# Two gate chunks of the latent branch as one block with seven products in six of its pairs

## The chip, the cores and the metric

The kernel runs on one core of one Trainium2 chip. The metric is the device time of one execution in microseconds (us). Three runs of the kernel before give a median of 1937.64 us (1937.38 to 1937.88). The engines are TensorE (PE, with its weight loads as PEld), VectorE (DVE), ScalarE (ACT), GpSimd (POOL) and SyncE (SP), which issues most loads.

## The reference

The kernel is one layer of a bidirectional encoder on 256 rows of width 4096, in float32. One projection `w_in` gives everything that the two attention branches need; each branch has 16 heads of width 128.

```python
h = rms_norm(x, g_mix[i])
proj = jnp.einsum('bsd,de->bse', h, w_in[i])
c_q, c_kv, k_rope, gate_a, q_b, k_b, v_b, gate_b = jnp.split(proj, split_idx, axis=-1)
q_a = jnp.einsum('bsr,re->bse', rms_norm(c_q, g_q_latent[i]), w_uq[i])
...
kv = jnp.einsum('bsr,re->bse', rms_norm(c_kv, g_kv_latent[i]), w_ukv[i])
...
y_a = rms_norm(y_a.reshape(B, S, MLA_WIDTH), g_out_mla[i]) * jax.nn.silu(gate_a)
...
y_b = rms_norm(y_b.reshape(B, S, DIL_WIDTH).astype(x.dtype), g_out_dil[i]) * jax.nn.silu(gate_b)
x = x + jnp.einsum('bse,ed->bsd', jnp.concatenate([y_a, y_b], axis=-1), w_out[i])
ple = jnp.einsum('bsc,cd->bsd', p[i], w_ple[i])
gate = jax.nn.sigmoid(jnp.einsum('bsd,de->bse', rms_norm(x, g_ple[i]), w_ple_gate[i]))
x = x + ple * gate
```

Between the lines stand the latent attention (a rotary part of 64 columns, a dense softmax) and the dilated attention. `gate_a`, 2048 columns, is what the change is about.

## The kernel before

**Products in three passes.** Each float32 operand is split into a high and a low half (`split`, L112: ScalarE copies the high half at L115, VectorE subtracts for the low half at L116). `mm` (L130) makes one product of three matrix instructions, high by high, high by low, low by high (L133 to L135). The 256 rows are two halves t of 128. A weight chunk of 512 columns and 4096 rows is 32 row blocks (kt) of 128.

**Steps.** The matrix work is a list `steps`, in the order in which TensorE gets it. Each step has a load (SP), a split, and its products. An `Old` step is two row blocks of a chunk of up to 512 columns, for both halves of the rows: 12 matrix instructions. The main loop at the end issues, for each step i, the loads up to a few steps ahead, the splits (`convert`) up to two steps ahead (more where a block has a ring of more than three buffers), then the products of step i, and then calls `advance`.

**Tasks beside the steps.** What is not a weight product is a generator that is taken on by one `yield` per step in `advance`: first the list `urgent` (evacuations, statistics, gating), in the order of spawning, then up to five `running` attention heads. A head waits in `waiting` until its flag is set and two steps have passed since the last start. All engines work in program order, so what a task issues stands in each engine's queue between the splits of that step and those of the next.

**Blocks with seven products.** `Block` (L729) handles 1024 columns at once as a 2 by 2 product of halves of the rows and halves of the columns. Two row blocks (a pair) make either two plain steps, with four products per row block, or one fast pair of four steps: seven products per pair instead of eight, with sums of the weights made by VectorE at L780 and L796, and with sums of x prepared by `add_sums` (L812). The products collect in eight PSUM banks: M2, X, M3, M4 take the plain steps too, M1, M5, M6, M7 only the fast ones. When the last fast pair is done, a `mid` task combines M1, M5, M6, M7; when the last step is done, a `done` task adds M2, X, M3, M4. The order `CCCCSCSCSCSCSCSC` has a letter for each pair, C plain and S fast. The six dilated blocks (q, k, v, twice) and others use this already; the sums `x_s` for the dilated blocks are made late, after the latent heads.

**The order around the change.** First come four chunks of 400 columns (the latents and the rotary key, 64 steps, `done_a`); the last of them spawns `latents`, which turns the rotary key, and the flag "latents" is set when the latents are normalised. Then come gate chunk 0 (16 steps), and eight groups of eight steps: one step of gate chunk 1, four of `w_uq` (two heads' q), one of gate chunk 1, two of `w_ukv` (two heads' k and v). `done_uq` (L472) reads the PSUM banks of `w_uq` at L478, turns the rotary part on GpSimd and transposes it (L488); its last part sets the flag ("uq", i). `done_uk` (L498) reads k at L511 and v at L118 and L119, and puts two heads in `waiting`. `w_uq` and `w_ukv` share one pair of banks.

**A latent head** (`attend`, L386) takes nine steps: transposes of q and k (L393, L394), the split of both, the scores (ten matrix instructions into bank s, L133 to L135, L408, L409), the maximum and exponentials (L415, L417), the normalisation (L433, L438), transposes (L443), their split, the weighted sum into bank o, and its reading (L456, L458). Of the two heads of a group, this text calls the first A and the second B.

**The gate.** `done_gate` (L546) reads a finished gate chunk: a tanh (L550) and a product (L551) for each half of the rows. It then waits for the branch's 1/rms (`ry`, set by `y_stats` when all heads are done), scales, transposes (L564) and multiplies with the heads' outputs (L572). Chunks 2 and 3 of the gate follow the eight groups, 32 steps; in them the last heads end, `y_stats` and the gating run, and `x_sums` makes the sums of x for the dilated blocks.

Of the kernel before, what the change touches and what calls it, by code (L numbers as in the profile page):

```python
# [12 lines left out]
F32R = mybir.dt.float32r  # L13
I32 = mybir.dt.int32
AF = mybir.ActivationFunctionType
ALU = mybir.AluOpType
AX = mybir.AxisListType

P = 128
S = 256  # L20
NT = S // P
DM = 4096
HEADS = 16
# [6 lines left out]
OFF_GA = Q_LORA + KV_LORA + ROPE  # L30
# [48 lines left out]
def encoder_layer(ctx: ExitStack, tc: tile.TileContext, x, p, positions, g_mix, w_in, g_q_latent, w_uq,  # L79
                  g_kv_latent, w_ukv, g_out_mla, g_out_dil, w_out, w_ple, g_ple, w_ple_gate, g_final,  # L80
                  c_inv, c_dist, out):
    nc = tc.nc
    x, p, out = x[0], p[0, 0], out[0]
# [10 lines left out]
    def slot(tag, shape, dtype=F32):  # L94
        names[tag] = names.get(tag, 0) + 1
        return sp.tile([P, *shape], dtype, tag=tag, name=f"{tag}_{names[tag]}")
# [137 lines left out]
    flags, urgent, waiting, running = set(), [], [], []  # L234
    ticks = [0, -9]

    def spawn(task):
        urgent.append(task)
# [66 lines left out]
    T7 = {}  # L305
# [166 lines left out]
    def done_uq(i):  # L472
        def task(ps):
            q = slot("T5", [NT, 2, NOPE + ROPE])
            kq = slot("T6", [1024])
            pairs[i] = {"q": q, "kq": kq}
            for t in range(NT):
                nc.scalar.activation(q[:, t].rearrange("p h c -> p (h c)"), ps[t], AF.Copy, scale=rqs[:, t:t + 1])  # L478
            both = kq[:, 512:].rearrange("p (t h d r) -> p t h d r", t=NT, h=2, d=2)
            rotate(both[:, :, :, 0], q[:, :, :, NOPE:], both[:, :, :, 1], 2)  # L480
            yield
            yield
            nc.scalar.activation(both[:, :, :, 1], both[:, :, :, 0], AF.Copy)
            yield
            tp = turn_bank([2, S])
            for h in range(2):
                for t in range(NT):
                    nc.tensor.transpose(tp[:, h, t * P:(t + 1) * P], both[:, t, h].rearrange("p d r -> p (d r)"),  # L488
                                        ident)
            yield  # L490
            pe = slot("Q0", [2, S], F32R)
            nc.scalar.activation(pe, tp, AF.Copy)
            nc.vector.tensor_tensor(pe[ROPE:], tp[ROPE:], plain(pe[ROPE:]), op=ALU.subtract)
            pairs[i]["pe"] = pe
            flags.add(("uq", i))
        return task
# [28 lines left out]
    def lhs_c(key):  # L525
        return lambda kt: (cT[key][0][:, kt], cT[key][1][:, kt])
# [5 lines left out]
    def y_stats(dil):  # L532
        while not all(("head", dil, h) in flags for h in range(HEADS)):
            yield
        yield
        tp = turn_bank([2 * S])
        for t in range(NT):
            nc.tensor.matmul(tp[:, t:t + 1], acc[:, t * P:(t + 1) * P], ones, start=True, stop=True)
        yield
        yield from rsqrt_mean(ry[dil], tp[:, :NT], WIDTH)  # L540
        nc.vector.tensor_tensor(ry[dil], ry[dil], rxh, op=ALU.mult)
        flags.add(("ry", dil))

    U_TAGS = ("B7a", "B7b", "T5", "T6"), ("T7", "B7a", "B7b", "T4")

    def done_gate(dil, c):  # L546
        def task(ps):
            u = slot(U_TAGS[dil][c], [NT, 512])
            for t in range(NT):
                nc.scalar.activation(u[:, t], ps[t], AF.Tanh, scale=rxh[:, t:t + 1])  # L550
                nc.vector.scalar_tensor_tensor(u[:, t], u[:, t], 1.0, ps[t], op0=ALU.add, op1=ALU.mult)  # L551
                yield
            while ("ry", dil) not in flags or (c and ("turned", dil, c - 1) not in flags):
                yield
            yield
            for t in range(NT):
                nc.scalar.activation(u[:, t], u[:, t], AF.Copy, scale=ry[dil][:, t:t + 1])
            yield
            for b in range(2):
                w = u[:, :, S * b:S * (b + 1)]  # L560
                tp = turn_bank([2, S])
                for k in range(2):
                    for t in range(NT):
                        nc.tensor.transpose(tp[:, k, t * P:(t + 1) * P], w[:, t, k * P:(k + 1) * P], ident)  # L564
                if b:
                    flags.add(("turned", dil, c))
                yield
                for k in range(2):
                    h = 4 * c + 2 * b + k
                    g = G["ob" if dil else "oa"][:, h:h + 1]  # L570
                    y = yb_rows(h) if dil else by_token(y_rows(ya, h))
                    nc.vector.scalar_tensor_tensor(by_token(w[:, k]) if dil else y, y, g, by_token(tp[:, k]),  # L572
                                                   op0=ALU.mult, op1=ALU.mult)
            if not dil:
                flags.add(("gated", c))
                return
            while (("yT", 0, 3) if c == 0 else ("yT", 1, 1)) not in flags and c != 1:
                yield
            if c == 2:
                yt = [slot(b, [4, S], F32R) for b in ("B7a", "T6")]  # L580
            else:
                both = slot({0: "B3", 1: "B5", 3: "B6"}[c], [2, 4, S], F32R)
                yt = [both[:, 0], both[:, 1]]
            yT[4 + c] = yt
            for b in range(2):
                yield
                split(*(q[:, 2 * b:2 * b + 2] for q in yt), u[:, :, S * b:S * (b + 1)])
            flags.add(("yT", 1, c))
        return task

    def split_ya():
# [124 lines left out]
    WP = ["wp"] * 3  # L716
# [92 lines left out]
                Step(None, lambda hi, lo: split(hi, lo, T[1]), run(("M6", S(1)), ("M4", A22)), needs, 0),  # L809
            ]  # L810

    def add_sums(n, pair, dst, tmp, name, out):  # L812

        def task():
            def two(op, d, a, b):
                nc.vector.tensor_tensor(d, a, b, op=op)

            w = slot(tmp, [2, 8, P])  # L820
            for j in range(n):
                a, u = w[:, j % 2, :4], w[:, j % 2, 4:]
                hi, lo = (q.rearrange("p k (t c) -> p (k t) c", t=NT) for q in pair(j))
                two(ALU.add, a, plain(hi), plain(lo))
                two(ALU.add, u[:, 0], a[:, 1], a[:, 3])
                two(ALU.subtract, u[:, 1], u[:, 0], a[:, 0])
                two(ALU.subtract, u[:, 2], a[:, 1], a[:, 0])
                two(ALU.subtract, u[:, 3], a[:, 2], u[:, 1])
                yield
                d = dst(j)  # L830
                split(d[:, 0], d[:, 1], u)
                out[j] = [(d[:, 0, i], d[:, 1, i]) for i in range(4)]
                flags.add((name, j))
                yield
        return task()


# [249 lines left out]
    def banks():  # L1087
        turn[0] ^= 1
        return M[turn[0]]
# [3 lines left out]
    def add(ch, lo=0, hi=None):  # L1093
        steps.extend((ch, j) for j in range(lo, ch.nk // ch.per if hi is None else hi))

    def cols(w, lo, n):
        return w[:, lo:lo + n]

    def from_x(lo, n, done):
        return Chunk(cols(w_in, lo, n), 32, n, lhs_x, banks(), done)  # L1100

    for i in range(4):
        add(from_x(400 * i, 400, done_a(i)))
    add(from_x(OFF_GA, 512, done_gate(0, 0)))
    ga1 = from_x(OFF_GA + 512, 512, done_gate(0, 1))
    other = banks()
    for i in range(8):
        add(ga1, 2 * i, 2 * i + 1)
        add(Chunk(cols(w_uq, 384 * i, 384), 8, 384, lhs_c("q"), other, done_uq(i), lambda j: ["latents"]))
        add(ga1, 2 * i + 1, 2 * i + 2)  # L1110
        add(Chunk(cols(w_ukv, 512 * i, 512), 4, 512, lhs_c("kv"), other, done_uk(i), lambda j: ["latents"]))
    for c in (2, 3):
        add(from_x(OFF_GA + 512 * c, 512, done_gate(0, c)))
    hooks = {}
    EVEN, ODD = ("m0", "m1", "s", "o", "m2", "m3", "t0", "t1"), ("m2", "m3", "t0", "t1", "m0", "m1", "s", "o")
    LAST = "m2", "m3", "s", "o", "m0", "m1", "t0", "t1"
# [1 line left out]
    def mix(shape):  # L1118
        n = shape.count("S")
        fast, plain_ = iter(range(n)), iter(range(n, 16))  # L1120
        return [("ple", 0) if x == "e" else ("fast", next(fast)) if x == "S" else ("plain", next(plain_)) for x in shape]
# [18 lines left out]
    def hook(at, f):  # L1140
        assert at not in hooks
        hooks[at] = f

    def only(*tags):
        def go():
            turns[:] = tags
        return go

    x_s = {}
    z_tags = "T0", "T1", "T2", "T3", "T4", "T7"  # L1150

    def x_sums():
        while ("ry", 0) not in flags:
            yield
        yield from add_sums(6, lambda j: [q[:, 2 * (j % 4):2 * (j % 4) + 2] for q in xT[j // 4]],
                            lambda j: slot(z_tags[j], [2, 4, P], F32R), "B0", "x_sums", x_s)

    hook(64 + 16 + 64, lambda: spawn(y_stats(0)))
    hook(64 + 16 + 64 + 12, lambda: spawn(x_sums()))
    gated_rings = {("T4", "T7"): ("mid", ("k", 1)), "Al1": ("y_sums", FAST_O - 1)}  # L1160
    for n, key in enumerate((key, i) for i in range(2) for key in "qkv"):
        off = {"q": OFF_Q, "k": OFF_K, "v": OFF_V}[key[0]] + 1024 * key[1]
        order = mix("CCCCSCSCSCSCSCSC" if n < 5 else "CCCCCSCCSCCSCCSC")
# [202 lines left out]
    for i, step in enumerate(steps):  # L1366
# [23 lines left out]
        n = 0  # L1390
# [33 lines left out]
```

## Time and profile before

| | |
|---|---|
| median of three runs | 1937.64 us |
| the profiled execution | 1936.72 us |
| its span, first to last instruction | 1934.9 us |
| mean granted TensorE clock | 0.998 |
| VectorE busy | 1449.5 us (75%) |
| ScalarE busy | 1065.6 us (55%) |
| moved from HBM and back | 364.72 MB read, 4.19 MB written |

A row of the profile names the line, the engine, the operation, what it writes and reads (tile names without their numbers: m, s, o, t are PSUM banks, hi, lo the split weights, raw the loaded ones, Ah and Al the halves of x, B and T buffers in SBUF), and the shape. In a grouped row follow the count, the busy time with the mean in ns, and the idle time of the engine ahead of it with what ended it. In the timeline each row has start and duration. In the rows of waits stand the waiting instruction, an arrow, and what it waited for. Matrix instructions overlap, so their pace is read from the distance of their starts.

Seen in order of time, the four latent chunks end at about 155.6 us, gate chunk 0 follows, the first `w_uq` product starts at 203.2 us, the last one at 387.2 us.

### The profile page before, as it was taken

To read this page: it belongs to the slowest core of one execution; us is meant where nothing else is said; L and a number is where in the kernel's file an instruction comes from. 1 tells how busy PE (TensorE), PEld (TensorE's weight loads), DVE (VectorE), ACT (ScalarE), POOL (GpSimd) and SP (SyncE) were. 2 spreads that over 40 slices of the span, in tenths; PEclk is the share of its full clock that TensorE was granted. 3 is DMA by queue.
4 is the path that set the end of the run, shared out by engine and by line. 5 is a ranking of instruction groups with operands and counts; after the bars stand their busy time and mean duration, and the time that the engine had idled before them with its cause. 6 is when DMAs were issued, how large, how long until landed. Compare 5 with 4: busy or idle time off the path is not lost.

```text
span 1934.9 us, 25431 instructions
## 1 busy us (share of the span) xinstructions
PE 1918.6 (99%) x9335; PEld 1638.0 (85%) x9335; DVE 1449.5 (75%) x1973; ACT 1065.6 (55%) x1459; POOL 69.7 (4%) x124
## 2 busy tenths in 40 slices
PE   9999999999999999999999999999999999999997
PEld 8998899988888888888888888888888888888887
DVE  7645566667787887878677777888876598888765
ACT  6544555555554555545456666555555455655543
POOL 1001111110000000000000010000000000000000
PEclk9999999999999999999999999999999999999999
DMA  7666545445665656666664456665656566566655
GB/s 257 189 187 194 173 141 153 147 153 174 196 207 192 224 192 191 214 195 199 212 196 143 145 153 218 220 216 176 205 194 212 187 190 219 190 216 207 228 183 177
DMA packets 150572, 370.57 MB, mean 192 GB/s; under 512 B 11924, under 2 KB 45808, under 8 KB 150192
## 3 DMA queue, kind: packets, MB, share of 16 engines
q1 hardware_dynamic: 148528, 361.80, 58.5%
q0 software_dynamic: 1920, 7.15, 1.1%
q8 instruction: 73, 1.20, 0.2%
q14 instruction: 51, 0.42, 0.1%
HBM read 364.72 MB, written 4.19 MB: 191 GB/s over the span
## 4 chain that ended last, share of the span: by engine, by line
PE 98%; DVE 1%; ACT 0%; DMA 0%; issue 0%; SPq 0%; DVEq 0%; ACTq 0%
PE m L133 21%; PE m L134 21%; PE m L135 21%; PE t L133 4%; PE t L135 4%; PE t L134 4%; PE o L134 3%; PE o L135 3%; PE o L133 3%; PE s L134 3%; PE s L135 3%; PE s L133 3%; PE t L443 1%; PE t L393 0%; PE t L394 0%; PE t L564 0%
## 5 line engine op out<-in xcount | busy, mean ns | idle before, releaser
L116 DVE TENSOR_TENSOR lo<-raw,hi 128x1024 fp32r<-128x1024 f32 (+3 forms) x507 | 570.7, 1133 | 276.0 <-ACT hi L115 274.7
L115 ACT ACTIVATE hi<-raw 128x1024 fp32r<-128x1024 f32 (+3 forms) x507 | 496.8, 987 | 379.4 <-PE m L135 189.6
L133 PE MATMUL m<-hi,Ah 128*128 128x512 f32 (+2 forms) x1203 | 457.5, 380 | 0.4 <-ACT Ah L125 0.4
L134 PE MATMUL m<-lo,Ah 128*128 128x512 f32 (+2 forms) x1203 | 451.6, 375 | 0.2 <-DVE lo L116 0.2
L135 PE MATMUL m<-hi,Al 128*128 128x512 f32 (+2 forms) x1199 | 449.6, 375 | 0.0
L135 PEld LDWEIGHTS m<-hi,Al 128*128 128x128 f32 x1199 | 225.3, 188 | 36.1 <-DVE Al L127 0.2
L134 PEld LDWEIGHTS m<-lo,Ah 128*128 128x128 f32 x1203 | 226.4, 188 | 33.4 <-DVE lo L116 0.8
L133 PEld LDWEIGHTS m<-hi,Ah 128*128 128x128 f32 x1203 | 226.3, 188 | 33.4 <-ACT Ah L125 0.6
L133 PE MATMUL m<-hi,B 128*128 128x512 f32 (+1 forms) x403 | 153.8, 382 | 0.0
L135 PE MATMUL m<-hi,B 128*128 128x512 f32 (+1 forms) x403 | 150.1, 372 | 0.0
L134 PE MATMUL m<-lo,B 128*128 128x512 f32 (+1 forms) x403 | 149.9, 372 | 0.0
L116 DVE TENSOR_TENSOR B<-raw,B 128x1024 fp32r<-128x1024 f32 (+1 forms) x81 | 87.0, 1088 | 31.0 <-ACT B L115 30.9
L115 ACT ACTIVATE B<-raw 128x1024 fp32r<-128x1024 f32 (+1 forms) x81 | 75.7, 950 | 53.0 <-PE o L135 24.6
L135 PEld LDWEIGHTS m<-hi,B 128*128 128x128 f32 x403 | 75.7, 188 | 11.2
L134 PEld LDWEIGHTS m<-lo,B 128*128 128x128 f32 x403 | 75.9, 188 | 9.8
L133 PEld LDWEIGHTS m<-hi,B 128*128 128x128 f32 x403 | 75.8, 188 | 9.9
L116 DVE TENSOR_TENSOR T<-t,T 128x512 fp32r<-128x512 f32 (+1 forms) x65 | 44.4, 684 | 41.5 <-ACT T L115 41.2
L793 ACT ACTIVATE hi<-raw 128x1024 fp32r<-128x1024 f32 x44 | 46.9, 1065 | 50.1 <-PE t L135 20.7
L115 ACT ACTIVATE hi<-B 128x1024 fp32r<-128x1024 f32 x44 | 46.7, 1061 | 42.4 <-PE o L135 29.8
L133 PE MATMUL m<-B,Ah 128*128 128x512 f32 (+1 forms) x184 | 68.2, 371 | 0.0
L134 PE MATMUL m<-B,Ah 128*128 128x512 f32 (+1 forms) x184 | 68.2, 371 | 0.0
L135 PE MATMUL m<-B,Al 128*128 128x512 f32 (+1 forms) x184 | 68.2, 371 | 0.0
(693 smaller groups left out, 3546.2 us busy)
## 6 DMA issues: line engine op xcount, KB each, us to landing
raw<-in_w_in_dram SPq DMA_DIRECT2D x320, 512.0 KB, 3.8
raw<-in_w_out_dram SPq DMA_DIRECT2D x128, 512.0 KB, 4.5
raw<-in_w_ple_gate_dram SPq DMA_DIRECT2D x128, 512.0 KB, 4.6
raw<-in_w_in_dram SPq DMA_DIRECT2D x63, 400.0 KB, 3.2
raw<-in_w_uq_dram SPq DMA_DIRECT2D x32, 384.0 KB, 3.4
raw<-in_w_ukv_dram SPq DMA_DIRECT2D x16, 512.0 KB, 3.9
T<-in_x_dram SPq DMA_DIRECT2D x7, 512.0 KB, 5.1
T<-in_x_dram POOLq DMA_DIRECT2D x7, 512.0 KB, 6.9
```

The costliest lines, as they stand in the source:

```text
L115: nc.scalar.activation(hi, src, AF.Copy)
L116: nc.vector.tensor_tensor(lo, src, plain(hi), op=ALU.subtract)
L133: nc.tensor.matmul(ps, ah, bh, start=start, stop=False)
L134: nc.tensor.matmul(ps, ah, bl, start=False, stop=False)
L135: nc.tensor.matmul(ps, al, bh, start=False, stop=stop)
L443: nc.tensor.transpose(tp[:, k, t * P:(t + 1) * P], e[:, t, k * P:(k + 1) * P], ident)
L793: nc.scalar.activation(hi, r[1], AF.Copy)
```

## The change

Gate chunks 0 and 1 become one `Block` of 1024 columns that stands directly behind the latent chunks: 44 steps, of which 20 are plain (one row block each) and 24 belong to six fast pairs. Its sums of x (`x0_sums`) are made by a second call of `add_sums`, spawned at step 24, with two more idle steps per pair (`rest`), in buffers of their own. `gates_mid` and `gates_done` collect the block's products in the buffers of chunks 0 and 1 (B7a, B7b), apply the tanh and the product, and spawn the second half of the old `done_gate`, now `gating`.

A group of latent heads becomes seven steps: one of gate chunk 2, four of `w_uq`, two of `w_ukv`. The other half of gate chunk 2 and all of chunk 3 follow, 24 steps. Chunks 2 and 3 get fixed banks. `y_stats(0)` and `x_sums` are spawned at the first and second step behind the groups, and `x_sums` waits for the last head instead of for `ry`. `U_TAGS` and the dilated gates are as before.

```diff
-    def done_gate(dil, c):
-        def task(ps):
-            u = slot(U_TAGS[dil][c], [NT, 512])
-            for t in range(NT):
-                nc.scalar.activation(u[:, t], ps[t], AF.Tanh, scale=rxh[:, t:t + 1])
-                nc.vector.scalar_tensor_tensor(u[:, t], u[:, t], 1.0, ps[t], op0=ALU.add, op1=ALU.mult)
-                yield
+    def gating(dil, c, u):
+        def task():
             while ("ry", dil) not in flags or (c and ("turned", dil, c - 1) not in flags):
...
+    def done_gate(dil, c):
+        def task(ps):
+            u = slot(U_TAGS[dil][c], [NT, 512])
+            for t in range(NT):
+                nc.scalar.activation(u[:, t], ps[t], AF.Tanh, scale=rxh[:, t:t + 1])
+                nc.vector.scalar_tensor_tensor(u[:, t], u[:, t], 1.0, ps[t], op0=ALU.add, op1=ALU.mult)
+                yield
+            yield from gating(dil, c, u)
+        return task
+    QUARTERS = (0, 0, "M2"), (1, 1, "X"), (0, 1, "M3"), (1, 0, "M4")
+    def gates_mid(blk):
+        def task():
+            u = blk.u = [slot(U_TAGS[0][h], [NT, 512]) for h in range(2)]
+            ps = blk.ps
+            c11, c12, c21, c22 = u[0][:, 0], u[1][:, 0], u[0][:, 1], u[1][:, 1]
+            nc.scalar.activation(c11, ps["M1"], AF.Copy)
+            for d, a, m in ((c22, c11, "M6"), (c12, c22, "M5"), (c21, c22, "M7"), (c22, c21, "M5")):
+                nc.vector.tensor_tensor(d, a, ps[m], op=ALU.add)
+            yield
+        return task
+    def gates_done(blk):
+        def task():
+            for t, h, m in QUARTERS:
+                nc.vector.tensor_tensor(blk.u[h][:, t], blk.u[h][:, t], blk.ps[m], op=ALU.add)
+            w = slot("T4", [2, 512])
+            for old, new in ((), QUARTERS[:2]), (QUARTERS[:2], QUARTERS[2:]), (QUARTERS[2:], ()):
+                yield
+                for i, (t, h, m) in enumerate(old):
+                    q = blk.u[h][:, t]
+                    nc.vector.scalar_tensor_tensor(q, w[:, i], 1.0, q, op0=ALU.add, op1=ALU.mult)
+                for i, (t, h, m) in enumerate(new):
+                    nc.scalar.activation(w[:, i], blk.u[h][:, t], AF.Tanh, scale=rxh[:, t:t + 1])
+            for h in range(2):
+                spawn(gating(0, h, blk.u[h]))
+        return task
...
-    def add_sums(n, pair, dst, tmp, name, out):
+    def add_sums(n, pair, dst, tmp, name, out, rest=0):
...
-                yield
+                for _ in range(1 + rest):
+                    yield
...
-    add(from_x(OFF_GA, 512, done_gate(0, 0)))
-    ga1 = from_x(OFF_GA + 512, 512, done_gate(0, 1))
-    other = banks()
-    for i in range(8):
-        add(ga1, 2 * i, 2 * i + 1)
-        add(Chunk(cols(w_uq, 384 * i, 384), 8, 384, lhs_c("q"), other, done_uq(i), lambda j: ["latents"]))
-        add(ga1, 2 * i + 1, 2 * i + 2)
-        add(Chunk(cols(w_ukv, 512 * i, 512), 4, 512, lhs_c("kv"), other, done_uk(i), lambda j: ["latents"]))
-    for c in (2, 3):
-        add(from_x(OFF_GA + 512 * c, 512, done_gate(0, c)))
...
+    hook(24, lambda: spawn(add_sums(6, x_pair, z0_dst, ("B7a", "B7b"), "x0_sums", x0_s, 2)))
+    gated_rings = {("T4", "T7"): ("mid", ("k", 1)), "Al1": ("y_sums", FAST_O - 1), ("T5", "T6"): "kpe"}
+    order = mix("CCCCSCSCSCSCSCSC")
+    blk = Block(w_in[:, OFF_GA:OFF_GA + 1024], lhs_x, x0_s, "x0_sums", order, lambda kt: (), LAST, ("T2", "T3"),
+                WP + [("T5", "T6")])
+    lay(blk, order, gates_mid(blk), gates_done(blk))
+    ga2 = from_x(OFF_GA + 1024, 512, done_gate(0, 2))
+    ga2.banks, other = M
+    for i in range(8):
+        add(ga2, i, i + 1)
+        add(Chunk(cols(w_uq, 384 * i, 384), 8, 384, lhs_c("q"), other, done_uq(i), lambda j: ["latents"]))
+        add(Chunk(cols(w_ukv, 512 * i, 512), 4, 512, lhs_c("kv"), other, done_uk(i), lambda j: ["latents"]))
+    hook(len(steps), lambda: spawn(y_stats(0)))
+    hook(len(steps) + 1, lambda: spawn(x_sums()))
+    add(ga2, 8)
+    ga3 = from_x(OFF_GA + 1536, 512, done_gate(0, 3))
+    ga3.banks = M[1]
+    add(ga3)
...
     def x_sums():
-        while ("ry", 0) not in flags:
+        while ("head", False, HEADS - 1) not in flags:
             yield
...
-    hook(64 + 16 + 64, lambda: spawn(y_stats(0)))
-    hook(64 + 16 + 64 + 12, lambda: spawn(x_sums()))
```

More of the change, by code (lines that the diff above doesn't have):

```diff
@@ L588, in task @@
             flags.add(("yT", 1, c))
+        return task()
+    def done_gate(dil, c):
[32 more added lines that the diff above has]
+                spawn(gating(0, h, blk.u[h]))
         return task
@@ L818, in two @@
                 nc.vector.tensor_tensor(d, a, b, op=op)
-            w = slot(tmp, [2, 8, P])
+            if isinstance(tmp, tuple):
+                w = [slot(b, [8, P]) for b in tmp]
+            else:
+                both = slot(tmp, [2, 8, P])
+                w = [both[:, 0], both[:, 1]]
             for j in range(n):
-                a, u = w[:, j % 2, :4], w[:, j % 2, 4:]
+                a, u = w[j % 2][:, :4], w[j % 2][:, 4:]
                 hi, lo = (q.rearrange("p k (t c) -> p (k t) c", t=NT) for q in pair(j))
@@ L1147, in only, with z0_dst, x_pair @@
         return go
+    x0_s, z0 = {}, {}
+    def z0_dst(j):
+        if j < 4:
+            if j % 2 == 0:
+                both = slot(("B2", "B3")[j // 2], [2, 2, 4, P], F32R)
+                z0[j], z0[j + 1] = both[:, 0], both[:, 1]
+            return z0[j]
+        return slot(f"T{j - 4}", [2, 4, P], F32R)
+    def x_pair(j):
+        return [q[:, 2 * (j % 4):2 * (j % 4) + 2] for q in xT[j // 4]]
+    hook(24, lambda: spawn(add_sums(6, x_pair, z0_dst, ("B7a", "B7b"), "x0_sums", x0_s, 2)))
[16 more added lines that the diff above has]
+    add(ga3)
     x_s = {}
@@ L1152, in x_sums @@
     def x_sums():
-        while ("ry", 0) not in flags:
+        while ("head", False, HEADS - 1) not in flags:
             yield
-        yield from add_sums(6, lambda j: [q[:, 2 * (j % 4):2 * (j % 4) + 2] for q in xT[j // 4]],
-                            lambda j: slot(z_tags[j], [2, 4, P], F32R), "B0", "x_sums", x_s)
-    hook(64 + 16 + 64, lambda: spawn(y_stats(0)))
-    hook(64 + 16 + 64 + 12, lambda: spawn(x_sums()))
-    gated_rings = {("T4", "T7"): ("mid", ("k", 1)), "Al1": ("y_sums", FAST_O - 1)}
+        yield from add_sums(6, x_pair, lambda j: slot(z_tags[j], [2, 4, P], F32R), "B0", "x_sums", x_s)
     for n, key in enumerate((key, i) for i in range(2) for key in "qkv"):
```

## The prediction

> **What bounds the kernel now.** I read the first page, then who waited for whom, then stretches of the timeline. Beside each busy time stands its share.
>
> ```profile
> span 1934.9 us, 25431 instructions
> PE 1918.6 (99%) x9335; PEld 1638.0 (85%) x9335; DVE 1449.5 (75%) x1973; ACT 1065.6 (55%) x1459; POOL 69.7 (4%) x124
> PE 98%; DVE 1%; ACT 0%; DMA 0%; issue 0%; SPq 0%; DVEq 0%; ACTq 0%
> ```
>
> The chain that ended last is 98% TensorE. A full TensorE row could still hide pauses, because each row shows 0.39 us while the next product starts earlier. So I look for waits, and then at distances between starts.
>
> ```profile
> PEld s L134 <- DVE T L116: 1.6, 7, 0.2
> PE o L133 <- ACT T L115: 0.7, 1, 0.7
> PE o L134 <- DVE T L116: 0.3, 1, 0.3
> PEld m L134 <- DVE lo L116: 0.3, 1, 0.3
> ```
>
> Columns: total us, times, longest. The first row is from 228 to 396 us, the next two from 396 to 410, the last from 410 to the end: behind the start of the kernel, TensorE and its weight loads wait almost only inside the latent attention. Two places have a size. Head B of a pair waits for the low half of its q and k, seven times; once the weighted sum of a head comes late. The starts give the loss itself:
>
> ```profile
> 338.79 0.28 PE L133 MATMUL s<-T 128*128 128x256 f32 x1
> 338.98 0.39 PE L134 MATMUL s<-T 128*128 128x256 f32 x1
> 339.21 0.28 PE L135 MATMUL s<-T 128*128 128x256 f32 x1
> 339.32 0.27 PE L408 MATMUL s<-T,Q 128*128 128x256 f32 x1
> ...
> 400.40 0.39 PE L135 MATMUL m<-hi,Al 128*128 128x512 f32 x1
> 401.49 0.38 PE L133 MATMUL o<-T,B 128*128 128x256 f32 x1 [0.71 <-ACT T L115]
> 402.44 0.28 PE L135 MATMUL o<-T,B 128*128 128x256 f32 x1
> ```
>
> A 256-column product takes 0.12 us from start to start (339.21 to 339.32). From 338.79 to 339.21 stand two in 0.42 us: 0.18 lost, and seven times that is **1.26**. From 400.40 to 402.44 stand one of 512 columns (0.23, below) and two of 256 in 2.04: **1.57** lost. TensorE sets the pace everywhere else, so a product taken out is worth its full distance.
>
> **The block.** A gate chunk is 16 steps of 12 products, two are 384. The block has ten plain pairs (24 products each) and six fast ones (seven products of three, 21): 240 + 126 = 366, so 18 fewer. The dilated blocks have the same order of pairs; their last additions start at
>
> ```profile
> 581.98 1.40 DVE L651 SCALAR_TENSOR_TENSOR B<-m,st,B 128x512 f32<-128x512 f32 x2
> 664.94 0.74 DVE L651 SCALAR_TENSOR_TENSOR B7a<-m,st,B7a 128x512 f32<-128x512 f32 x1
> ```
>
> 82.96 us from block to block, over 366 products: 0.2267 us each, with no pause inside. The block gives 18 x 0.2267 = **-4.08**.
>
> The Trainium skill, "TensorE: Matmul & The Clock Gate", section "Wait — 56ns, not 53.3ns?", has 215.7 ns from start to start at 512 columns; by it this term would be -3.88. The trace differs, and 0.2267 is kept.
>
> **What lies beside TensorE.** The loads are 32 of 512 KB as before, on SP in step order; only their shape changes, to that of the dilated blocks. VectorE takes over most of the new work:
>
> ```profile
> 66.00:119.00 53.00, 53.00 (x298) 52.90 (x297) 29.04 (x46) 25.84 (x39) 0.00 (x0) 1.00 0.63 186
> 155.90:198.00 42.10, 42.10 (x192) 34.81 (x192) 24.89 (x50) 18.64 (x26) 5.45 (x11) 1.00 0.62 187
> 581.98:664.94 82.96, 82.96 (x368) 68.69 (x367) 68.72 (x78) 44.38 (x46) 0.00 (x0) 1.00 0.62 203
> ...
> L116 DVE TENSOR_TENSOR lo<-raw,hi 128x1024 fp32r<-128x1024 f32 x12 | 14.3, 1220 | 4.3 <-ACT hi L115 4.3
> ...
> L818 DVE TENSOR_TENSOR B<-B 128x128 f32<-128x128 f32 x24 | 5.9, 287 | 0.4
> L818 DVE TENSOR_TENSOR B<-Ah,Al 128x512 f32<-128x512 f32 x6 | 4.1, 684 | 0.0
> L116 DVE TENSOR_TENSOR T<-B,T 128x512 fp32r<-128x512 f32 x6 | 4.1, 681 | 0.0
> ...
> L551 DVE SCALAR_TENSOR_TENSOR B7b<-B7b,m x2: 678/681/684, 391.6 to 394.1; 128x512 f32<-128x512 f32 x2
> ```
>
> Each window row has the stretch, its length, then PE, PEld, DVE, ACT and POOL. The extra sums of x are the three groups from L818 on: 5.9 + 4.1 + 4.1 = 14.1 us of VectorE, spread over 24 steps from step 24 on, about 66 to 119 us (298 products there, some 12 to a step). VectorE goes from 29.0 to 43.1 of 53 us there, ScalarE gains six activations of 512 columns (about 3.6, at 0.60 each, a row further down). The conversions are two steps ahead, so I cost it at nothing; uncovered it would be those 14.1 us. In the block itself VectorE has 68.7, less nine additions of d_mid and d_done (9 x 0.74 = 6.7), plus the eight of the gate quarters (at L551's 0.68, 5.4), plus what the end of the latents leaves (24.89 less 16 conversions of 1.22: 5.4): 72.8 of 82.96 us. Tight but below, and the fixed part falls in the eight plain steps ahead of the first fast pair. Zero. Tanh and its product stay four of each.
>
> **The latent heads.** A group is now one gate step, four of w_uq, two of w_ukv: seven steps instead of eight. Both chunks use the same two banks and the gate step that stood between them is gone, so the first product of w_ukv waits for ScalarE to read w_uq's banks:
>
> ```profile
> 211.38 0.33 PE L135 MATMUL m<-hi,B 128*128 128x384 f32 x1
> 211.55 0.39 PE L133 MATMUL m<-hi,Ah 128*128 128x512 f32 x1
> ...
> 211.29 1.05 ACT L478 ACTIVATE T<-m,st 128x384 f32<-128x384 f32 x2 [0.56 <-PE m L135]
> ...
> L478 ACT ACTIVATE T<-m,st 128x384 f32<-128x384 f32 x16 | 8.8, 582 | 15.6 <-PE m L135 15.6
> ...
> 338.24 0.69 DVE L116 TENSOR_TENSOR T<-t,T 128x512 fp32r<-128x512 f32 x1 [2.83 <-ACT T L115]
> ```
>
> TensorE is free for the next product at 211.55, the first bank has been read at 211.29 + 0.58 = 211.87; with 0.05 for the handover (a split's end, 338.24 + 0.69, to the product at 338.98 that waited for it) that is 0.37 us. The second bank (212.34) is ready before its three products later. So **0.37** for group 0. From group 1 on, heads are in flight. A pair starts when ("uq", i) is set, which comes in the second step of the next group, so head A starts after the group's third step, head B after its fifth, which is w_uq's last. At exactly that point TensorE gets A's ten score products, B's first four transposes and the previous B's weighted sum:
>
> ```profile
> 332.29 0.28 PE L133 MATMUL s<-T 128*128 128x256 f32 x1
> 333.48 0.27 PE L393 MATMUL t<-ident,T 128*128 128x128 f32 x1
> 333.83 0.42 PE L133 MATMUL m<-hi,B 128*128 128x384 f32 x1
> ```
>
> Ten score products take 1.19, four transposes 0.35, the six products of the sum at the scores' distance 0.71: 2.25 us, and the second reading ends 0.79 us behind w_uq (212.34 less 211.55). Covered; if it were not, 0.37 in each of the other seven, 2.6 more.
>
> The seven waits of head B:
>
> ```profile
> L417 ACT ACTIVATE T<-s,st 128x256 f32<-128x256 f32 x28 | 13.0, 471 | 17.5 <-DVE st L415 17.5
> L415 DVE TENSOR_REDUCE st<-s 128x2 f32<-128x512 f32 x14 | 9.6, 683 | 0.0
> L115 ACT ACTIVATE T<-t 128x512 fp32r<-128x512 f32 x29 | 17.4, 599 | 0.0
> L115 ACT ACTIVATE hi<-raw 128x1024 fp32r<-128x1024 f32 x36 | 37.6, 1065 | 21.2 <-PE m L135 19.7 <-issue 1.5
> ```
>
> Now B's split stands on ScalarE behind the reading of w_uq and A's two exponentials, all in one step, and has one gate step (2.72 us, 12 x 0.2267) before its scores. In the new order they are a step apart. From the end of w_uq: reading until 0.79, a conversion (1.06) until 1.9, VectorE's half of it (1.22) until 3.2, A's maximum (0.68) until 3.9, exponentials (about 0.95) until 4.9, B's split (0.60 and 0.69) until 6.2. TensorE comes to B's scores at 2.25 + 2 x 2.72 = 7.7. A margin of 1.5 us, so I take -1.26; the other end is 0.
>
> The late weighted sum:
>
> ```profile
> L438 DVE TENSOR_SCALAR T<-T,st 128x256 f32<-128x256 f32 x28 | 8.6, 351 | 0.5
> ...
> 397.40 1.23 DVE L116 TENSOR_TENSOR lo<-raw,hi 128x1024 fp32r<-128x1024 f32 x1 [2.04 <-ACT hi L115]
> 398.55 0.47 DVE L511 TENSOR_SCALAR T<-m,st 128x256 f32<-128x256 f32 x1
> 401.47 0.69 DVE L116 TENSOR_TENSOR T<-t,T 128x512 fp32r<-128x512 f32 x1
> ```
>
> The tanh and the two 0.68 products of chunk 1 (391.6 to 394.1) push VectorE back just as k and v of the last group are read (2.92 us, 398.55 to 401.47), and the split that the sum needs stands behind both. With the change this gate work is done before the heads begin, and that of chunk 2 comes eight steps behind the last w_ukv step, where no k and v follow. So -1.57, the other end 0. What is late next is A's normalisation, which now stands behind k and v: 2.92 plus two of 0.35 (L438) and a reciprocal, some 3.8, against 1.19 of B's scores, 2.72 of a gate step and 0.35 of transposes, 4.3: it holds, by 0.5.
>
> **Behind the heads** 24 steps are left instead of 32. Counted in steps behind the last w_ukv: head 15 done at 13, 1/rms at 18, the four gatings three steps each, until 31; the dilated block claims a transposing bank at 34. The sums of x start at 13 and end at 25, the block wants the first at 32. Zero.
>
> **Sum.** -4.08 - 1.26 - 1.57 + 0.37 = -6.54. The profiled execution took 1936.72 us (span 1934.9), the median is 0.92 above it: 1937.64 - 6.54 = **1931.1**.
>
> **Rivals.** (1) *The waits come back* one link further on: only -4.08 + 0.37, 1933.9. For it: margins of 1.5 and 0.5 us; against it, nothing in the new order stands more densely than in the old. (2) *The handover is bare in all eight groups*: 2.6 more, 1933.7. For it: the same two banks in succession; against it, the 2.25 us above. The Trainium skill, "Perfetto Trace Analysis", section "Matmuls", asks that independent groups of products rotate through different banks, so that one is read while the next runs; by that rule this rival is what happens. No row here has such a succession. (3) *VectorE sets the block's pace* and eats all of the 4.08: 1935.2. Against it: 72.8 of 82.96. (4) *Slower*: at the handover the two readings stand behind a conversion that is itself late, so that each group pays 0.37 + 1.06 = 1.43 instead of the cover: 8 x 1.43 - 0.37 = 11.1 more, **1942.2**. It is slower than before from 0.86 us in each group on ((6.54 + 0.37) / 8). For it: ScalarE is in order, and its share per time rises as a step without attention work goes; against it, the reading at 211.29 found ScalarE idle for 0.56 us. That the change does not do what it says would need the sums not to be ready; they are spread over 24 steps and end 16 before the block.
>
> **How the numbers follow.** Forecast 0.72, rivals 0.10, 0.06, 0.05, 0.07. 0.2%, about what a measurement of this kernel tells from no change, is 3.9 us: 1933.8. Faster is the forecast and somewhat under half of rivals 1 and 2, which end on that line: 0.79; same 0.14; slower 0.07. The low end: no handover loss (-6.91) and 0.6 for smaller delays among the heads, 1930.1, with the scatter of the runs shown 1929.8. The high end takes in rivals 1 and 2 and 0.7 more, 1934.6.
>
> **What would show it.** The block's 366 products in 83 us and no TensorE wait in it; no more rows of s waiting for DVE T and o for ACT T; one gap of 0.3 to 0.4 us ahead of the first w_ukv product, and none in later groups; a group shorter by 2.72 + 0.18 = 2.90 us. It is wrong if waits of m for ACT T L478 (its line moves) appear eight times, if lo or the raw differences hold TensorE in the block, or if the dilated block stops at its first fast pair.

## The result, and the profile after

| | before | after |
|---|---|---|
| median, us (runs) | 1937.46 (5) | 1946.98 (5; 1945.75 to 1947.50) |
| the profiled execution, us | 1936.72 | 1946.98 |
| its span, us | 1934.9 | 1944.7 |

The medians were taken on one chip, kernel beside kernel: the ratio is 1.0047, 95% interval 1.0033 to 1.0062. The changed kernel is slower by 9.5 us, where 6.5 less had been forecast; 1946.98 lies outside the range, above even the slower rival's 1942.2.

The first view to read is again who waited for whom, for TensorE, after the change (columns: total us, times, longest):

```profile
PE o L134 <- DVE T L116: 5.5, 7, 0.9
PE m L133 <- ACT T L478: 3.9, 7, 0.6
PE t L270 <- DVE lo L116: 1.6, 1, 1.6
...
PE m L134 <- DVE lo L832: 0.5, 1, 0.5
PE t L443 <- DVE T L438: 0.3, 1, 0.3
```

The row of s waiting for DVE T is gone, and so is the late sum of before. In their place stand two that repeat with the groups: the first `w_ukv` product (m, L133) waits for the reading of `w_uq`'s banks (ScalarE, L478; the line has not moved), and the low half of a weighted sum (o, L134) waits for a split on VectorE. Starts on TensorE show what each costs. The timeline at the first kind, in group 4:

```profile
344.97 0.33 PE L135 MATMUL m<-hi,B 128*128 128x384 f32 x1
345.14 0.28 PE L133 MATMUL o<-T,B 128*128 128x256 f32 x1
...
347.05 0.27 PE L393 MATMUL t<-ident,T 128*128 128x128 f32 x1
347.16 0.27 PE L394 MATMUL t<-ident,T 128*128 128x128 f32 x1
347.27 0.27 PE L393 MATMUL t<-ident,T 128*128 128x128 f32 x1
347.38 0.27 PE L394 MATMUL t<-ident,T 128*128 128x128 f32 x1
348.21 0.50 PE L133 MATMUL m<-hi,B 128*128 128x512 f32 x1 [0.56 <-ACT T L478]
348.55 0.39 PE L134 MATMUL m<-lo,B 128*128 128x512 f32 x1
```

A transpose takes 0.11 from start to start, so from 347.38 to 348.21 are lost 0.72; the first product after the pause takes 0.34 instead of 0.23, 0.11 more. Together 0.83, in each of seven groups. And at the second kind:

```profile
362.88 0.28 PE L133 MATMUL o<-T,B 128*128 128x256 f32 x1
364.03 0.39 PE L134 MATMUL o<-T,B 128*128 128x256 f32 x1 [0.87 <-DVE T L116]
364.25 0.28 PE L135 MATMUL o<-T,B 128*128 128x256 f32 x1
```

Two distances of 1.15 and 0.22 where 0.12 each is the pace: 1.13 lost, six times. The seventh wait of that row is smaller and stands in the tail, where another 1.1 is lost in a few places (432 to 464 us).

Why the reading is so late is one row of ScalarE. First after, then before (its transposes at 333.48 stand in the prediction):

```profile
347.58 1.05 ACT L478 ACTIVATE T<-m,st 128x384 f32<-128x384 f32 x2 [3.25 <-PE t L393]
```

```profile
335.70 1.10 ACT L478 ACTIVATE T<-m,st 128x384 f32<-128x384 f32 x2 [2.15 <-PE m L135]
```

Before, the reading was released by the product that filled its bank (PE m). After, it is released by a *transpose* (PE t, L393), and starts at 347.58, 0.31 behind the start of the last L393 (347.27), though the banks had been full since 345.1. The output T is the buffer T5, of which there is one. The new q is written where the q of the pair before lies, and head B of that pair reads it in two of those four transposes (L393; L394 reads its k). Before, they came at 333.48, 2.2 us ahead of the reading; now they come behind `w_uq`, and the reading, though issued first, waits for them.

The sum, from starts on TensorE:

| place | us |
|---|---|
| forecast and found: 18 products, seven waits of s, the late sum | -4.08 - 1.26 - 1.57 |
| handover in group 0 (forecast 0.37) | +0.42 |
| handover in seven groups, 0.83 each | +5.8 |
| weighted sums, six of 1.13, and the tail's 1.1 | +7.9 |
| first two fast pairs of the block | +1.0 |
| ahead of the first gate product (155.73 before, 157.51 after; see the last section) | +1.8 |
| together | +10.0 |

The spans differ by 9.8. The block itself is where it was expected; these are its first and last starts and the first of `w_uq`:

```profile
157.51 0.40 PE L133 MATMUL m<-hi,Ah 128*128 128x512 f32 x1
...
245.27 0.39 PE L135 MATMUL m<-hi,Al 128*128 128x512 f32 x1
245.50 0.33 PE L133 MATMUL m<-hi,B 128*128 128x384 f32 x1
```

From 157.51 to 245.50 stand the 366 products, 12 of the first step of gate chunk 2 and ten transposes of the latents: 378 x 0.2267 + 10 x 0.11 = 86.8. The rest of the 87.99 is the pause of 1.0 at 191 to 194 us and two first products after a transpose, 0.1 each.

### The profile page after: what moved, and what is told of

It reads as the page before. It is cut to its first block, busy times and chain, and to the rows that moved or that the text cites. A ratio compares the mean times of both kernels' runs of the same rounds, so it can differ in the third digit from the quotient of the medians.

```text
span 1944.7 us, 25491 instructions
## 1 busy us (share of the span) xinstructions
PE 1918.8 (99%) x9317; PEld 1636.6 (84%) x9317; DVE 1487.4 (76%) x2053; ACT 1079.2 (55%) x1478; POOL 81.6 (4%) x124
## 4 chain that ended last, share of the span: by engine, by line
PE 96%; DVE 2%; ACT 1%; DMA 0%; issue 0%; SPq 0%; DVEq 0%; ACTq 0%
PE m L133 20%; PE m L134 20%; PE m L135 20%; PE t L133 4%; PE t L135 4%; PE t L134 4%; PE o L134 4%; PE o L135 4%; PE o L133 4%; PE s L133 3%; PE s L135 3%; PE s L134 3%; PE t L443 1%; DVE lo L116 1%; ACT hi L115 0%; DMA raw<-in_w_in_dram 0%
## 5 line engine op out<-in xcount | busy, mean ns | idle before, releaser
L116 DVE TENSOR_TENSOR lo<-raw,hi 128x1024 fp32r<-128x1024 f32 (+4 forms) x495 | 552.4, 1127 | 255.9 <-ACT hi L115 254.7
L115 ACT ACTIVATE hi<-raw 128x1024 fp32r<-128x1024 f32 (+4 forms) x495 | 482.4, 982 | 330.0 <-PE m L135 138.4
L133 PE MATMUL m<-hi,Ah 128*128 128x512 f32 (+2 forms) x1118 | 423.8, 379 | 0.0
L134 PE MATMUL m<-lo,Ah 128*128 128x512 f32 (+2 forms) x1118 | 419.0, 375 | 0.7 <-DVE lo L832 0.5
L135 PE MATMUL m<-hi,Al 128*128 128x512 f32 (+2 forms) x1114 | 416.7, 374 | 0.0
L134 PEld LDWEIGHTS m<-lo,Ah 128*128 128x128 f32 x1118 | 210.8, 189 | 31.5 <-DVE lo L116 1.2
L135 PEld LDWEIGHTS m<-hi,Al 128*128 128x128 f32 x1114 | 209.8, 188 | 32.5 <-DVE Al L127 0.2
L133 PEld LDWEIGHTS m<-hi,Ah 128*128 128x128 f32 x1118 | 210.8, 189 | 29.6
L133 PE MATMUL m<-hi,B 128*128 128x512 f32 (+1 forms) x405 | 154.2, 381 | 4.1 <-ACT T L478 3.9
L134 PE MATMUL m<-lo,B 128*128 128x512 f32 (+1 forms) x405 | 150.7, 372 | 0.0
L133 PEld LDWEIGHTS m<-hi,B 128*128 128x128 f32 x405 | 76.1, 188 | 16.1 <-ACT T L478 6.1
L134 PEld LDWEIGHTS m<-lo,B 128*128 128x128 f32 x405 | 76.2, 188 | 10.3 <-DVE lo L116 0.2
L829 ACT ACTIVATE hi<-raw 128x1024 fp32r<-128x1024 f32 x50 | 53.2, 1065 | 54.7 <-PE o L135 22.5
L133 PE MATMUL m<-B,Ah 128*128 128x512 f32 (+1 forms) x184 | 68.5, 372 | 0.0
L134 PE MATMUL m<-B,Ah 128*128 128x512 f32 (+1 forms) x184 | 68.2, 371 | 0.0
```

The costliest lines, as they stand in the source:

```text
L115: nc.scalar.activation(hi, src, AF.Copy)
L116: nc.vector.tensor_tensor(lo, src, plain(hi), op=ALU.subtract)
L133: nc.tensor.matmul(ps, ah, bh, start=start, stop=False)
L134: nc.tensor.matmul(ps, ah, bl, start=False, stop=False)
L135: nc.tensor.matmul(ps, al, bh, start=False, stop=stop)
L829: nc.scalar.activation(hi, r[1], AF.Copy)
```

## The experiments

**Theory A**: the single buffer T5 makes the reading wait for head B's transposes; ScalarE, in order, passes this on as late conversions, exponentials and splits, and the late weighted sums are its second effect. **Rival B**: it is the bank handover itself, two chunks in succession on the same two banks. **Rival C** is a late signal that `w_uq` is done in the expectations of the first two runs, and in that of the third it is the rotation on GpSimd, which reads q's rotary part and so could hold the buffer. **Rival D**, in the fourth run, is that the block and its sums cost time on the whole, through VectorE; in the fifth A and D are about the pauses in the block alone.

**Two halves for q.** The 128 plain columns of q go into one tile for all pairs, with two halves used in turn. The rotary 64 columns go into an unused half of the scratch tile (the squares of the latent heads move to its other half). There are four readings instead of two.

```diff
-            q = slot("T5", [NT, 2, NOPE + ROPE])
+            if i == 0:
+                pairs["q"] = slot("T5", [2, NT, 2, NOPE])
+            q = pairs["q"][:, i % 2]
...
+            rope = junk[:, S:].rearrange("p (t h r) -> p t h r", t=NT, h=2)
...
-                nc.scalar.activation(q[:, t].rearrange("p h c -> p (h c)"), ps[t], AF.Copy, scale=rqs[:, t:t + 1])
+                src = ps[t].rearrange("p (h c) -> p h c", h=2)
+                nc.scalar.activation(q[:, t], src[:, :, :NOPE], AF.Copy, scale=rqs[:, t:t + 1])
+                nc.scalar.activation(rope[:, t], src[:, :, NOPE:], AF.Copy, scale=rqs[:, t:t + 1])
-            rotate(both[:, :, :, 0], q[:, :, :, NOPE:], both[:, :, :, 1], 2)
+            rotate(both[:, :, :, 0], rope, both[:, :, :, 1], 2)
```

> The changed kernel, but the part of q that head transposes read lies in two alternating buffers (both inside T5), and the rotary part of q goes to a half of junk; the two reads of w_uq's banks become four. Nothing else moves: same steps, same banks, same order on TensorE. Theory A (the reading of w_uq at L478 must not overwrite T5 before the last head of the pair before has transposed its q out of it, and those transposes now stand in the same step; everything behind on ScalarE waits with it): the seven waits ahead of w_ukv (0.84 us each) and the waits of the weighted sum (1.12 us each) vanish, 14.6 us in all less a few tenths for the two more reads, so 1932 to 1934 us, against 1947 of the changed kernel. Rival B (two chunks in succession on the same two PSUM banks): the waits ahead of w_ukv stay at 0.4 to 0.8 us in each group, 1937 to 1946 us. Rival C (the signal that w_uq is done reaches ScalarE only with a later product, whatever the buffers): both kinds of waits stay, 1946 to 1948 us.

Measured: 1932.39 us (nine runs) against 1937.53, ratio 0.9974, interval 0.9964 to 0.9983; span 1930.3. That is 14.4 of span less than the changed kernel, and faster than the kernel before. From the same view as above, three rows of TensorE's waits (the last one is a wait at 12 us, in the kernel's start):

```profile
PE m L134 <- DVE lo L837: 0.5, 1, 0.5
PE m L133 <- ACT junk L483: 0.3, 1, 0.3
PE m L134 <- DVE lo L116: 0.2, 1, 0.2
```

Both repeated rows are gone together. L483 is the handover of group 0; one short wait of a sum, 0.3 by its starts, is left. The handover in the timeline of group 4, with the first reading on ScalarE and the second product of the next weighted sum:

```profile
338.58 0.48 ACT L482 ACTIVATE T<-m,st 128x256 f32<-128x256 f32 x1 [0.50 <-PE m L135]
...
340.69 0.28 PE L409 MATMUL s<-T,Q 128*128 128x256 f32 x1
...
341.14 0.27 PE L394 MATMUL t<-ident,T 128*128 128x128 f32 x1
341.17 0.48 PE L133 MATMUL m<-hi,B 128*128 128x512 f32 x1
341.48 0.39 PE L134 MATMUL m<-lo,B 128*128 128x512 f32 x1
...
355.84 0.28 PE L134 MATMUL o<-T,B 128*128 128x256 f32 x1
```

`w_ukv` follows the last transpose at once, on the same two banks as in the changed kernel. B falls for groups 1 to 7. So does C, the late signal: the reading is again released by the product that fills its bank (PE m), and starts at 338.58, before the last product of `w_uq` (338.73).

**One half only.** The same, but each pair uses half 0. Since the tile is not handed out anew, the program orders reading and transposes as they are issued: head B of each pair but the last works on the next pair's q, and the output is not that of the layer.

```diff
-            q = pairs["q"][:, i % 2]
+            q = pairs["q"][:, 0]
```

> As split_q, but with one buffer for q instead of two in turn: one index differs. It carries the four reads and the moved rotary part and puts the reuse of the buffer back. Theory A: within 1.5 us of the changed kernel, 1945.5 to 1949 us, the reading of w_uq again starting right behind the transposes of q. Rivals B and C: within 1 us of split_q, since neither knows this buffer.

Measured: 1931.86 us (five runs), ratio 0.9968 (0.9956 to 0.9981). A expected the waits back, at 1945.5 or more, and they did not come; the time is the one that B and C gave. The expectation had overlooked that without a new allocation nothing orders the reading behind transposes issued after it: there is no wait where the old q isn't kept. So this run does not test A: it uses one buffer, but without the order that A blames. Another was made.

**The buffer handed out anew.** Everything of the first experiment (four readings, the rotary part in its own place), but T5 allocated for each pair, with q's old value kept until its last reader.

```diff
-            if i == 0:
-                pairs["q"] = slot("T5", [2, NT, 2, NOPE])
-            q = pairs["q"][:, i % 2]
+            q = slot("T5", [NT, 2, NOPE])
```

> As split_q (q's 128 columns in one buffer, the rotary 64 in another, four readings per pair instead of two), but the buffer for q is handed out anew for each pair, so that it is the same memory as that of the pair before and is ordered behind all its readers. Theory A (the reading of w_uq's banks waits until head B of the pair before has transposed the old q): the handover gaps of 0.84 us come back in groups 1 to 7 and the late weighted sums of 1.1 us in six or seven, 12 us together, so 1944 to 1949, with a ratio of 1.0035 to 1.006. Theory B (the same two banks used in succession are the cause, and the smaller reading or the rotary part's own place is what helped split_q): no handover gap, within 1 us of split_q, 1931.5 to 1933.5. Theory C (the second half of the buffer helps only by giving the rotation on GpSimd more room): the same as B, since the rotation has its own buffer here too.

Measured: 1948.57 us (four runs), ratio 1.0056 (1.0042 to 1.0070), span 1946.9. TensorE's waits and the reading on ScalarE:

```profile
PE o L134 <- DVE T L116: 5.4, 7, 0.9
PE m L133 <- ACT junk L481: 5.3, 8, 0.7
```

```profile
348.41 0.47 ACT L480 ACTIVATE T<-m,st 128x256 f32<-128x256 f32 x1 [3.25 <-PE t L393]
348.78 0.36 ACT L481 ACTIVATE junk<-m,st 128x128 f32<-128x128 f32 x1
```

Both kinds of waits are back, with the same 3.25 us of idle ScalarE and the same releaser, and the time is inside A's range. C, the rotation, falls: it has its own buffer here. Against the first experiment only the buffer of q differs, and it is worth 16.6 us of span. Against the run with one half, which also writes each q over the one before, only the order behind the old q's readers is new, and it is worth 16.8 (1930.1 to 1946.9). The four shorter readings end a little later than two, so that this handover costs 0.99 by starts instead of 0.83.

**The order without the block.** Gate chunks 0 and 1 as plain chunks ahead of the groups, no early sums of x, groups of seven steps and the tail as in the change. The banks' turn is shifted by one, so that the groups get the banks that they have in the change.

```diff
-    turn = [0]
+    turn = [1]
...
-    hook(24, lambda: spawn(add_sums(6, x_pair, z0_dst, ("B7a", "B7b"), "x0_sums", x0_s, 2)))
-    lay(blk, order, gates_mid(blk), gates_done(blk))
+    add(from_x(OFF_GA, 512, done_gate(0, 0)))
+    add(from_x(OFF_GA + 512, 512, done_gate(0, 1)))
```

> The new order of the latent heads without the block: gate chunks 0 and 1 stay plain chunks of 16 steps each ahead of the groups, no extra sums of x. Theory A puts the whole loss into the groups and counts the block as a gain: 18 products more (+4.08), the block's own waits for VectorE gone (-1.0, and -0.3 in the latent chunks), one wait of up to 2 us where the first w_uq chunk needs the banks of gate chunk 1: 1949.5 to 1952.5 us. Rival D (the block and its sums cost time, through VectorE): faster than the changed kernel, 1937 to 1946 us.

Measured: 1949.39 us (four runs), ratio 1.0062 (1.0046 to 1.0077), span 1947.5. The waits are those of the change (o for DVE T 5.4 in seven, m for ACT T L478 4.4 in eight), and the kernel is 2.8 of span longer than the change. D falls, and the loss lies in the order of the groups. The time is 0.1 below A's range: the wait for the banks of gate chunk 1, for which A had allowed up to 2 us, did not come, and nothing is lost ahead of the first `w_uq` product. The block by itself gains 3.0: from the first gate product to the first of `w_uq` are 90.99 us here (156.22 to 247.21) and 87.99 in the change. That is the 4.08 less the pause of 1.0.

**The block's first fast pair later.** The first experiment with one more plain pair ahead of the first pair of seven products; the number of each kind is the same.

```diff
-    order = mix("CCCCSCSCSCSCSCSC")
+    order = mix("CCCCCSCSCSCSSCSC")
```

> As split_q, with the block's first fast pair one pair later (order CCCCCSCSCSCSSCSC, again ten plain and six fast pairs, so the same 366 products). Theory A (the two pauses of 0.8 and 0.2 us in the block come because the latents' small statistics instructions on VectorE fall into the first fast pairs, which want VectorE's sums of the weights): the pauses at the first two fast pairs go, 1.0 us less than split_q, 1931.0 to 1931.9, and no VectorE wait of TensorE in the block. Rival D (VectorE is too dense in any fast pair of this block): the pauses stay or move to where two fast pairs follow each other, 1932 to 1934.

Measured: 1932.26 us (eight runs), ratio 0.9973 (0.9962 to 0.9983): no gain, and inside D's range. In the timeline the pauses at the first two fast pairs are gone, as A had it, and one of 1.3 us (1.23 and 0.11) stands where two fast pairs follow each other, as D had it:

```profile
220.43 0.39 PE L135 MATMUL m<-T,Al 128*128 128x512 f32 x1
220.66 0.39 PE L133 MATMUL m<-hi,Ah 128*128 128x512 f32 x1
222.11 0.50 PE L134 MATMUL m<-lo,Ah 128*128 128x512 f32 x1 [1.06 <-DVE lo L837]
222.45 0.39 PE L135 MATMUL m<-hi,Al 128*128 128x512 f32 x1
```

A second fast pair right behind the first thus stops TensorE as well: VectorE has little to spare in any. That the latents' statistics are what tips the first two is not shown by this run: they still stand beside these pairs on VectorE (176 to 191 us), and what is new is the lead that one more plain pair gives it.

## Why the prediction was wrong

**The step that failed** is the word "Covered" at the handover in groups 1 to 7. The prediction listed the right work there (A's scores, B's four transposes, the sum before it: 2.25 us) and set it against a reading that would end 0.79 behind `w_uq`. It asked which bank the reading *reads*, and not which buffer it *writes*. The cover was the very thing that the reading waits for: it starts when the cover ends. Its time on ScalarE was then built on this 0.79. The list of that step, from the end of `w_uq` (last start plus 0.17), beside the first experiment's and the changed kernel's. ScalarE and VectorE with two halves for q, where `w_uq`'s last product starts at 338.73:

```profile
339.57 0.38 ACT L483 ACTIVATE junk<-m,st 128x128 f32<-128x128 f32 x1
339.82 1.07 ACT L115 ACTIVATE hi<-raw 128x1024 fp32r<-128x1024 f32 x1
...
343.61 0.20 ACT L417 ACTIVATION_READ_ACCUMULATOR T<-s,st 128x1 f32 x1
```

```profile
340.92 1.23 DVE L116 TENSOR_TENSOR lo<-raw,hi 128x1024 fp32r<-128x1024 f32 x1 [1.58 <-ACT hi L115]
342.06 0.69 DVE L415 TENSOR_REDUCE st<-s 128x2 f32<-128x512 f32 x1
344.33 0.69 DVE L116 TENSOR_TENSOR T<-t,T 128x512 fp32r<-128x512 f32 x1 [1.58 <-ACT T L115]
...
354.97 0.69 DVE L116 TENSOR_TENSOR T<-t,T 128x512 fp32r<-128x512 f32 x1
```

and in the changed kernel, where it starts at 344.97:

```profile
348.52 1.06 ACT L115 ACTIVATE hi<-raw 128x1024 fp32r<-128x1024 f32 x1
...
352.30 0.20 ACT L417 ACTIVATION_READ_ACCUMULATOR T<-s,st 128x1 f32 x1
```

```profile
349.61 1.23 DVE L116 TENSOR_TENSOR lo<-raw,hi 128x1024 fp32r<-128x1024 f32 x1 [4.03 <-ACT hi L115]
350.75 0.68 DVE L415 TENSOR_REDUCE st<-s 128x2 f32<-128x512 f32 x1
353.02 0.69 DVE L116 TENSOR_TENSOR T<-t,T 128x512 fp32r<-128x512 f32 x1 [1.58 <-ACT T L115]
...
363.28 0.69 DVE L116 TENSOR_TENSOR T<-t,T 128x512 fp32r<-128x512 f32 x1
```

| ends behind `w_uq`, us | predicted | two halves | change |
|---|---|---|---|
| reading | 0.8 | 1.0 | 3.5 |
| conversion, ScalarE | 1.9 | 2.0 | 4.4 |
| conversion, VectorE | 3.2 | 3.2 | 5.7 |
| A's maximum | 3.9 | 3.8 | 6.3 |
| A's exponentials | 4.9 | 4.9 | 7.4 |
| B's split | 6.2 | 6.1 | 8.6 |
| split for the weighted sum | - | 16.8 | 18.8 |

With the wait gone every predicted end holds to 0.3 us; with it, each is some 2.4 later than without. The last row is the second half of the loss: with two halves TensorE reaches the low product of the sum at 355.84, 0.2 behind the end of this split (355.66). In the change the split comes 2.07 later; TensorE, itself held up by the handover, comes 0.83 later, and 0.18 was slack. That leaves 1.06, and with the 0.10 lost at the product behind it 1.16, against the 1.13 seen. The waits at o are one effect with the handover, as the two experiments in which both go and come together show.

The other steps:

- **The block, -4.08**: right in its products and their pace. "The fixed part falls in the eight plain steps ahead of the first fast pair. Zero" was mis-sized by 1.0. The fixed part does not end there: the latents' statistics are issued a few instructions per step and reach into the first fast pairs. That they are the cause is likely by their amount and place, but no run takes them out. On VectorE in the first experiment they look like this, each 0.15 to 0.17 long and 0.2 apart, and between 180.9 and 192 there are 22 of them, some 4 us:

```profile
184.10 0.15 DVE L229 SCALAR_TENSOR_TENSOR st<-st 128x2 f32<-128x2 f32 x1
184.29 0.16 DVE L230 TENSOR_TENSOR st<-st 128x2 f32<-128x2 f32 x1
184.49 0.16 DVE L231 SCALAR_TENSOR_TENSOR st<-st 128x2 f32<-128x2 f32 x1
```

  The stretches of the changed kernel (length, then PE, PEld, DVE busy) show how full VectorE is: 21.31 of 22 us around the pause, 39.26 of 44 behind it. An average of 72.8 in 83 had hidden this. Rival 3 named the right engine and took four times its size.

```profile
178.00:200.00 22.00, 21.48 (x94) 17.17 (x93) 21.31 (x49) 12.13 (x13) 0.00 (x0) 1.00 0.60 182
200.00:244.00 44.00, 44.00 (x196) 36.44 (x195) 39.26 (x46) 24.47 (x27) 0.00 (x0) 1.00 0.62 196
```

- **The seven waits, -1.26, and the late sum, -1.57**: both gone, in every kernel with q in two halves and, for these causes, in the change as well. The margin of 1.5 at B's split is down to 0.1 in the change (the split ends at 353.71, B's scores start at 353.79); with the buffer handed out anew and in the order without the block, weight loads of s wait for DVE T again, 1.4 us in seven and 1.0 in five.
- **The handover in group 0, +0.37**: 0.42 measured, 0.57 with four readings.
- **A's normalisation, "holds by 0.5"**: it held everywhere but once, in the tail (0.3 by the view of waits), where all was late.
- **Rival 2, a bare handover in all groups**: right in its place, wrong in its cause. The Trainium skill, "Perfetto Trace Analysis", section "Matmuls", asks that independent groups of products rotate through banks. With two halves for q the same banks follow each other without a pause wherever 2.25 us of other products stand between, and with 0.57 where none do, in group 0.
- **Rival 4, slower**, had the right sign and a near mechanism, a reading that is late on ScalarE. It made the reading late by a conversion ahead of it, where it was the first in its queue and held up all the others, and it had no second effect on the sums: 1.43 a group instead of 0.83 + 1.13.
- **Ahead of the block** the early sums of x were put at nothing, and a pause of 0.3 at 86 us stands beside them; it is not there in the order without the block, which has no early sums. Another 1.5 of the 1.8 lost there was not forecast at all, and the last section shows that most of it differs from kernel to kernel where the work does not.
- **Behind the heads, zero**: the small losses in the tail (1.1) come with the late heads; from 470 to 620 us no pause over 0.12 is seen, before or after, so the dilated block does not stop.

The forecast of 1931.1 is met to 1.3 us by the kernel with two halves (1932.4), in part by luck. Its known differences from the forecast's sum are the pause in the block (1.0), the larger handover in group 0 (0.2), one wait of a sum (0.3) and a start that is later by 1.2 in its profile: 2.7 in all, where the span misses the sum by 1.9 (4.6 gained for 6.54). Where the other 0.8 was gained was not traced.

## What to carry to other kernels

When a step is moved, ask of each instruction that it issues not only whose output it reads, but who still reads the memory that it writes: a buffer of which there is one orders the writer behind all readers of the old value, even readers that are issued after it. Work that is counted as cover must be checked for this, because a cover that the covered instruction waits for is no cover. One such wait on an in-order engine was charged twice here, at the handover and, some 15 us later, at the next chain with no slack (0.2 us).

## What was not expected of the hardware

The first 24 steps of the changed kernel issue what they issued before, yet the first gate product came 1.8 us later than before in its profile. The five kernels that share the early sums of x do the same work up to there, and in their profiles, one execution each, this product starts at 156.19 (the first fast pair later), 156.79 (one half only), 156.93 (two halves), 157.07 (the buffer handed out anew) and 157.51 (the change), against 155.73 before and 156.22 in the order without the block, without early sums. So 1.3 us of difference stand between kernels that do the same work there, and the 1.8 is a figure of this profile more than of the change. The longest wait of a transpose of x at the kernel's start, 1.63 in the change and 0.98 before, does not go with it: it is 1.42 with two halves and 0.65 with one half only, which start their first gate product 0.14 apart. What sets this start was not tried.
